# Third head group of a dilated attention kernel: rotated q and k kept in token order, score products read with a step of sixteen words

## The chip, the cores and the metric

The kernel runs on one core of a Trainium2 chip. The metric is the device time of one execution in microseconds (us); the time of a kernel is the median of its runs. A core has TensorE (PE, with its weight loads shown as PEld), VectorE (DVE), ScalarE (ACT), GpSimd (POOL) and SyncE (SP, which here only issues DMAs), and sixteen DMA engines shared by all queues.

## The reference

The reference is one decoder block with two token mixers. Branch A, which the change touches, is causal dilated attention with three head groups of eight heads (head width 64) over 2048 positions. Cut to what matters:

```
DILATION_GROUPS = ((128, 1), (512, 4), (2048, 16))     # (window, dilation)
q = rope(q); k = rope(k)                               # absolute positions 0..2047
for g, (window, dilation) in enumerate(DILATION_GROUPS):
    # positions are regrouped by residue modulo dilation; within a residue
    # the pattern is a band, in blocks of 128 queries
    s = einsum('brnqhd,brnkhd->brnhqk', q_blocks, [previous block, this block] of k) * 64 ** -0.5
    p = exp(s - max(s)); o = p @ v / sum(p)
attn = sum over groups of softmax(log denominators) * o
```

For the third group (dilation 16) a residue has 2048 / 16 = 128 positions, which is one block without a previous one: sixteen blocks per head, each of 128 queries against 128 keys, whose positions lie sixteen apart. All values are float32. Branch B (a gated linear recurrence), the gates, the output projections and the layer norm are as before and after.

## The kernel before, in words

The work has four stages: the input projections (about 0 to 1463 us of the profiled span), the attention (to 1677 us), the projections of both branches, and the output with the layer norm.

**First stage.** The product `x @ W_in` is computed in 72 feature tiles of 128 columns and four token chunks of 512, two feature tiles at a time ("a plan" of pairs, run once for each half of the tokens, by a seven-product scheme on 2x2 blocks). Every float32 operand is split into a high and a low part that TensorE takes at full pace, so each block product is twelve matmuls of 128x512 (L597). `product` and `evacuate` are called once per tick, a tick being one block product. Everything that follows a feature tile (rotation of q and k, gates, recurrence) is a Python generator, a "chain", that gives up control with `yield Ask(...)`. `run_chains` resumes a chain when its lag in ticks is over, when enough of the 32 slots for 128x512 tiles are vacant (`need`), and when the engine budgets of this tick (`DVE=1.2` and the like) are not spent. So numbers in an `Ask` decide in which tick, and therefore in which place of each engine's stream, the work behind it is put. Engines work through their streams in order.

`qk_chain` does the rotation. SP swaps 32-row pieces into `sw`, DVE multiplies by the cosine, POOL by the sine, and a DVE add gives the rotated tile. For the first group the add works in place (`rp = rw`). For groups two and three (`g` is 1 and 2) it writes a new tile `rp`, with the words regrouped by residue: for the third group word `r * 32 + j` of a chunk holds position `16 * j + r`. A rotated k then goes to its scratch array (`k_scr`) as it is. A rotated q is scaled by 0.125 and split into `hi` (ACT) and the remainder (DVE), and both parts go to `qh_scr` and `ql_scr`. For the third group these two DMAs (L331) also gather a residue's words over the four chunks, so that 128 consecutive words of the array are one block; each of their 2048 pieces is 32 words. SP issues them, as it does the loads of the weights (`wA`, `wS`), the stores and loads of the weights' low parts (`wl_scr`, L278 and L283) and the pieces for the rotation (L303).

**Second stage.** There are twelve units, a unit being a pair of heads of one group, in the order group one, group three, group two, four times over. A unit has four iterations `i`, each of four blocks. `unit_parts` loads q's two parts into `A` and k into `B`, and splits k there into its high and low part. An iteration issues on TensorE: 24 score products (L976: four blocks, the three part products high-high, low-high and high-low, two heads on the two halves of the partitions), then the transposes of the previous iteration's probabilities (L1001), then the value products of the iteration before that (L1029). DVE adds the mask and takes the maximum (L983), ACT takes the exponential (L991), and ACT and DVE bring the transposed probabilities from PSUM (L1014, L1016). For the third group the block of q is `A[hs, x, n * P:(n + 1) * P]`, 128 consecutive words, and the block of k is four runs of 32 consecutive words, one of each chunk. These products have 128 moving columns; those of the first group, and most of the second, have 256.

Of the kernel before, what the change touches and what calls it, by code (L numbers as in the profile page):

```python
# [11 lines left out]
ALU = mybir.AluOpType  # L12
# [3 lines left out]
P = 128  # L16
# [4 lines left out]
CH = 512  # L21
# [10 lines left out]
def hybrid_block_kernel(ctx: ExitStack, tc: tile.TileContext, a: dict, out: bass.AP):  # L32
    nc = tc.nc
    sp, act, dve, pool, pe = nc.sync, nc.scalar, nc.vector, nc.gpsimd, nc.tensor

    def flat(t):
        return t.bitcast(F32)
# [14 lines left out]
    qk_scr = {(n, u): dram.tile([P, S], F32, name=f"{n}_scr{u}") for u in range(12) for n in ("qh", "ql", "k")}  # L52
# [77 lines left out]
    def take(name, dt=F32R):  # L130
        if not vacant:
            raise RuntimeError(f"no slot at {now['n']}: {[x[1].name if hasattr(x[1],'name') else x[1] for x in home.values()]} chains {len(chains)}")
        i = vacant.pop(0)
        t = sl_p.tile([P, CH], dt, tag=f"s{i}", name=name)
        home[id(t)] = (i, t)
        return t

    def give(*ts):
        for t in ts:
            vacant.append(home.pop(id(t))[0])  # L140

    def give_sent(*ts):

        for t in ts:
            later(2, lambda t=t: give(t))
# [69 lines left out]
    def tt(eng, out, in0, in1, op):  # L215
        eng.tensor_tensor(out=out, in0=in0, in1=in1, op=op)  # L216
# [71 lines left out]

    CS = {}

    def blocks(t, g):

        return t.rearrange("p (r j) -> p j r", r=4 if g == 1 else 16)

    def qk_chain(rw, f, c):
        isq = f < FT_K
        u = f % 12
        g = u // 4
        nm = f"{f}_{c}"
        yield Ask(need=1)  # L300
        sw = take("sw" + nm)
        for b in range(4):
            sp.dma_start(flat(sw)[32 * b:32 * b + 32], flat(rw)[32 * (b ^ 1):32 * (b ^ 1) + 32])  # L303
        yield Ask(lag=2, DVE=1.2 if c < 2 else 1.0, POOL=1.7)
        cos, sin = CS[c % 2]
        tt(dve, flat(rw), flat(rw), cos, ALU.mult)
        tt(pool, flat(sw), flat(sw), sin, ALU.mult)
        yield Ask(lag=1, need=1 if g else 0, DVE=1.2 if g else 1.0)
        if g == 0:
            rp = rw  # L310
            tt(dve, flat(rp), flat(rw), flat(sw), ALU.add)
            give(sw)
        else:
            rp = take("rp" + nm)
            v, r = "p (j r) -> p j r", 4 if g == 1 else 16
            tt(dve, blocks(flat(rp), g), flat(rw).rearrange(v, r=r), flat(sw).rearrange(v, r=r), ALU.add)
            give(rw, sw)
        if not isq:
            yield Ask()
            sp.dma_start(qk_scr["k", u][:, c * CH:(c + 1) * CH], flat(rp))  # L320
            give_sent(rp)
            return
        yield Ask(need=1, ACT=.66, DVE=.9)
        hi = take("hi" + nm)
        act.activation(hi, flat(rp), AF.Copy, scale=0.125)  # L325
        dve.scalar_tensor_tensor(out=rp, in0=flat(rp), scalar=0.125, in1=flat(hi), op0=ALU.mult, op1=ALU.subtract)
        yield Ask()
        for t, part in ((hi, "qh"), (rp, "ql")):
            dst = qk_scr[part, u]
            if g == 2:  # L330
                sp.dma_start(dst.rearrange("p (r i) -> p r i", r=16)[:, :, 32 * c:32 * c + 32],  # L331
                             flat(t).rearrange("p (r i) -> p r i", r=16))
            else:
                sp.dma_start(dst[:, c * CH:(c + 1) * CH], flat(t))
        give_sent(hi, rp)


# [209 lines left out]
    def result(s, fi, c, bank, u):  # L547
# [10 lines left out]
        if kind in ("qk", "v"):  # L558
            y = take("y" + nm)
            total(flat(y), bank, u, f, sgn, True)  # L560
            start_chain(qk_chain(y, f, c) if kind == "qk" else v_chain(y, sgn, f, c))
        elif kind == "mg":
            y = take("y" + nm, F32)
            total(y, bank, u, f, sgn, False)
            start_chain(mg_chain(y, sgn, f, c))
        elif kind == "ga" or not fi:
            y = take("y" + nm, F32)
            total(y, bank, u, f, sgn, False)
            start_chain(silu_chain(y, sgn, f, c))
        else:  # L570
            i = f - FT_U
            if c == 1 and i in put_off:
                y = take("y" + nm, F32)
                total(y, bank, u, f, sgn, True)
                act.activation(ubs[:, i, 2, 0:3], y[:, CH - 3:CH], AF.Copy)
                start_chain(store_chain(y, u_scr[i]))
                return
            ub = ub_free.pop(0)
            total(ub[:, 3:3 + CH], bank, u, f, sgn, True)
            start_chain(lru(i, c, ub), 7 if c % 2 else 0)  # L580
# [98 lines left out]
    for s, pl in enumerate(plan):  # L679
        if pl[0] and pl[4] == "ug":  # L680
            i = pl[1][1][0] - FT_U
# [79 lines left out]
    def unit(u):  # L761

        return (0, 2, 1)[u % 3], u // 3
# [152 lines left out]
    n = len(where)  # L916
# [30 lines left out]
    def first(i, j):  # L947
        u, q = divmod(i, 4)
        g, _ = unit(u)
        return 0 if prev(g, 4 * q + j) is not None else P  # L950

    def scores(i):
        u, q = divmod(i, 4)
        g, _ = unit(u)
        A, B = units[u]
        if q == 0:
            sta[u] = p_p.tile([P, 16, 4], F32, tag="sta", name=f"sta{u}", bufs=3)
            ot[u] = at_p.tile([P, S], F32, tag="ot", name=f"ot{u}")
        for w in range(2):
            s = st["s", i, w] = [aps.tile([P, 2, 256], F32, tag="s", name=f"s{i}{w}{h}", bufs=4) for h in range(2)]  # L960
            for j in range(2):
                n = 4 * q + 2 * w + j
                lo = first(i, 2 * w + j)
                for x, y in ((0, 0), (1, 0), (0, 1)):
                    for h, hs in enumerate(HALF):
                        K = B[hs, y]
                        if g == 2:
                            k = K.rearrange("p (c r j) -> p r c j", c=4, r=16)[:, n]
                        elif lo:
                            k = K[:, n * P:(n + 1) * P]  # L970
                        elif g == 0:
                            k = K[:, (n - 1) * P:(n + 1) * P]
                        else:
                            c, r = divmod(n, 4)
                            k = K[:, (c - 1) * CH:(c + 1) * CH].rearrange("p (c r j) -> p r c j", c=2, r=4)[:, r]
                        pe.matmul(s[h][:, j, lo:256], A[hs, x, n * P:(n + 1) * P], k, start=(x + y == 0), stop=(y == 1))  # L976

    def peak(i, j, h):
        u, q = divmod(i, 4)
# [111 lines left out]
    for i in range(NG + 3):  # L1091
        u = i // 4
# [9 lines left out]
        if on:  # L1102
            scores(i)
# [193 lines left out]
    for n in range(32):  # L1297
        c, f = divmod(n, 8)
# [147 lines left out]
    for tt in range(16):  # L1446
        c, b = divmod(tt, 4)
# [71 lines left out]
```

## Time and profile before

| | |
|---|---|
| median of three runs | 2148.55 us (2148.51 to 2153.36) |
| the profiled execution's own time | 2152.92 us |
| its span, first to last instruction | 2151.2 us |
| mean granted TensorE clock | 0.996 |
| PE busy | 2101.0 us (98%) |
| PEld busy | 1747.2 us (81%) |
| DVE busy | 1697.1 us (79%) |
| ACT busy | 1081.1 us (50%) |
| POOL busy | 738.4 us (34%) |
| DMA | 525.74 MB in 348266 packets, 123568 of them under 512 B |
| chain that ended last | PE 61% of the span, ACT 6%, DMA 5%, DVE 4% |

Busy time is the union of an engine's instructions. Matmuls overlap, so a matmul's duration in a row is longer than the time from one to the next. In the groups, a row gives busy time and mean duration of one, then the engine's idle time before them and who ended it; a row of a line or a tile gives the least, the median and the greatest duration.

### The profile page before, as it was taken

The numbers are of one execution on the slowest core, as the hardware profiler recorded it, in microseconds if no ns is written. First come the engines' busy times: TensorE is split into PE (matmuls) and PEld (weight loads), VectorE is DVE, ScalarE is ACT, GpSimd is POOL, SyncE is SP. The second block draws the span as 40 slices with busy tenths as digits, with TensorE's granted clock in tenths as the row PEclk, the third lists the DMA queues.
The fourth block names the chain that finished last, engine by engine and source line by source line (L and its number), as shares of the span: only waits on it lengthen the run. The fifth ranks groups of instructions, "written<-read, shape, count | busy, mean of one in ns | idle before, by whom it ended". The sixth has DMA issues, their size and how long they took to land.

```text
span 2151.2 us, 36029 instructions
## 1 busy us (share of the span) xinstructions
PE 2101.0 (98%) x12016; PEld 1747.2 (81%) x12016; DVE 1697.1 (79%) x3009; ACT 1081.1 (50%) x2284; POOL 738.4 (34%) x581
## 2 busy tenths in 40 slices
PE   8999999999999999999999999999999999979998
PEld 6888877888888888888888888887888888868887
DVE  8788888989989977787787887878999545466667
ACT  6354545456356566546657666658999211211100
POOL 1545454654654202121221231224446244321120
PEclk9999999999999999999999999999999999999999
DMA  8888897997997976677788878779898788954431
GB/s 271 255 263 251 249 262 223 271 275 245 279 288 240 306 225 192 221 233 221 233 258 268 267 243 257 244 243 382 284 312 266 232 265 278 306 186 142 164 108 69
DMA packets 348266, 525.74 MB, mean 244 GB/s; under 512 B 123568, under 2 KB 156336, under 8 KB 344240
## 3 DMA queue, kind: packets, MB, share of 16 engines
q1 hardware_dynamic: 330368, 491.64, 70.8%
q0 software_dynamic: 10080, 18.35, 5.4%
q10 hardware_dynamic: 7632, 13.44, 1.8%
q8 instruction: 96, 1.57, 0.3%
q14 instruction: 90, 0.74, 0.1%
HBM read 318.18 MB, written 190.45 MB: 236 GB/s over the span
## 4 chain that ended last, share of the span: by engine, by line
PE 61%; ACT 6%; DMA 5%; DVE 4%; issue 1%; SPq 1%; POOL 0%; DVEq 0%; ACTq 0%; POOLq 0%
PE q L597 39%; ACT p L991 5%; PE z L1389 3%; PE z L1387 3%; PE z L1388 3%; PE yb L1276 2%; PE yb L1277 2%; PE yb L1278 2%; PE o L1029 1%; ACT ptb L1014 1%; PE ya L1354 1%; PE ya L1355 1%; PE ya L1356 1%; PE s L976 1%; DMA yb_scr<-gB 1%
## 5 line engine op out<-in xcount | busy, mean ns | idle before, releaser
L597 PE MATMUL q<-xT,hS 128*128 128x512 f32 x1680 | 519.0, 390 | 0.0
L597 PE MATMUL q<-xT,l 128*128 128x512 f32 x1120 | 436.0, 389 | 0.0
L597 PE MATMUL q<-xB,hA 128*128 128x512 f32 x1248 | 387.4, 391 | 6.3 <-ACT xB L204 5.6
L597 PEld LDWEIGHTS q<-xT,hS 128*128 128x128 f32 x1680 | 314.1, 188 | 64.7 <-ACT hi L325 0.2
L597 PE MATMUL q<-xB,l 128*128 128x512 f32 x904 | 353.5, 391 | 1.2 <-DMA l<-wl_scr 1.1
L597 PEld LDWEIGHTS q<-xB,hA 128*128 128x128 f32 x1248 | 234.0, 188 | 56.2 <-ACT xB L204 5.6
L597 PEld LDWEIGHTS q<-xT,l 128*128 128x128 f32 x1120 | 210.2, 188 | 43.9
L597 PEld LDWEIGHTS q<-xB,l 128*128 128x128 f32 x904 | 170.3, 188 | 38.0 <-DMA l<-wl_scr 1.5
L216 POOL TENSOR_TENSOR S<-S,wA 128x512 f32<-128x512 f32 x35 | 45.7, 1306 | 414.4 <-DVE S L216 333.7
L216 POOL TENSOR_TENSOR sw<-sw,sin 128x512 f32<-128x512 f32 x96 | 161.4, 1687 | 73.8 <-DMA sw<-y 60.8
L261 ACT ACTIVATE hA<-wA 128x512 fp32r<-128x512 f32 x218 | 135.6, 624 | 90.2 <-DMA wA<-in_w_in_dram 41.1
L597 PE MATMUL q<-xB,hS 128*128 128x512 f32 x560 | 174.8, 393 | 3.0 <-DVE v L216 3.0
L597 PE MATMUL q<-xT,hA 128*128 128x512 f32 x560 | 173.3, 390 | 2.4 <-ACT hi L325 1.0
L991 ACT ACTIVATE p<-p,sta 128x256 f32<-128x256 f32 (+1 forms) x384 | 172.1, 455 | 4.6 <-DVE sta L983 3.9
L261 ACT ACTIVATE hS<-S 128x512 fp32r<-128x512 f32 x175 | 109.1, 624 | 92.7 <-DVE S L216 50.2
L216 POOL TENSOR_TENSOR l<-wA,hA 128x512 fp32r<-128x512 f32 x68 | 106.0, 1558 | 80.2 <-ACT hA L261 65.2
L597 PEld LDWEIGHTS q<-xT,hA 128*128 128x128 f32 x560 | 104.6, 188 | 26.1 <-issue 1.4
L597 PEld LDWEIGHTS q<-xB,hS 128*128 128x128 f32 x560 | 104.5, 189 | 25.1 <-issue 4.1
L983 DVE CUSTOM_DVE_ANT_0 p<-s,mask 128x256 f32<-128x256 f32 (+1 forms) x384 | 118.7, 361 | 4.3 <-PE s L976 3.6
L1360 POOL TENSOR_TENSOR me<-gA,ybr 128x512 f32<-128x512 f32 x32 | 51.2, 1610 | 194.6 <-DVE gA L1359 179.8
L216 DVE TENSOR_TENSOR y<-y,cos 128x512 f32<-128x512 f32 x96 | 103.9, 1088 | 16.3 <-DMA sw<-y 16.1
L1389 PE MATMUL z<-wo,ml 128*128 128x512 f32 (+1 forms) x264 | 102.0, 386 | 4.7 <-DVE ml L1373 4.7
(201 smaller groups left out, 4430.1 us busy)
## 6 DMA issues: line engine op xcount, KB each, us to landing
wA<-in_w_in_dram SPq DMA_DIRECT2D x253, 256.0 KB, 4.9
wl_scr<-l SPq DMA_DIRECT2D x105, 512.0 KB, 4.8
l<-wl_scr SPq DMA_DIRECT2D x105, 512.0 KB, 4.9
sw<-y SPq DMA_DIRECT2D x384, 64.0 KB, 3.1
wS<-in_w_in_dram SPq DMA_DIRECT2D x70, 256.0 KB, 4.6
wS<-in_w_in_dram POOLq DMA_DIRECT2D x70, 256.0 KB, 6.3
qh_scr<-hi SPq DMA_DIRECT2D x48, 256.0 KB, 5.1
v_scr<-vs SPq DMA_DIRECT2D x48, 256.0 KB, 4.5
```

The costliest lines, as they stand in the source:

```text
L216: eng.tensor_tensor(out=out, in0=in0, in1=in1, op=op)
L261: act.activation(h, r, AF.Copy)
L597: pe.matmul(bank, w[:, ks], x[:, kk, xx], start=(first and i == 0), stop=(last and i == 11))
L983: dve.tensor_tensor_reduce(out=st["p", i, j][:, h, lo:256], in0=st["s", i, j // 2][h][:, j % 2, lo:256], in1=mask[:, lo:256], scale=1.0, s ...
L991: act.activation(p, p, AF.Exp, scale=-1.0, bias=s[:, h:h + 1], accum_out=s[:, 2 + h:3 + h])
L1276: pe.matmul(yb, WL[f][:, 0, k], xx[:, 0], start=(k == 0), stop=False)
L1277: pe.matmul(yb, WL[f][:, 0, k], xx[:, 1], start=False, stop=False)
L1278: pe.matmul(yb, WL[f][:, 1, k], xx[:, 0], start=False, stop=(k == 7))
L1360: pool.tensor_tensor(out=ME[c][:, f], in0=ga, in1=yb, op=ALU.add)
L1387: pe.matmul(z, mh[:, k], w[:, 0, hs], start=(k == 0), stop=False)
L1388: pe.matmul(z, mh[:, k], w[:, 1, hs], start=False, stop=False)
L1389: pe.matmul(z, ml[:, k], w[:, 0, hs], start=False, stop=(k == 7))
```

## The change

The change is confined to the third group (`g == 2`).

- `qk_chain`: the rotated q and k are no longer regrouped. The add works in place, as for the first group, so there is no tile `rp`; the resumption before it asks for no vacant slot and a DVE budget of 1.0 instead of 1.2. `blocks` falls away, its case for the second group being written out.
- The DMAs of q's two parts write whole rows of 512 words into the scratch arrays; line L331 is gone. What `k_scr`, `qh_scr` and `ql_scr` hold is now in token order.
- `scores`: both operands of the third group's products are read with a step of sixteen words: 128 words of `A` and 128 words of `B`, each word 64 bytes from the last.

```
-        yield Ask(lag=1, need=1 if g else 0, DVE=1.2 if g else 1.0)
-        if g == 0:
+        yield Ask(lag=1, need=1 if g == 1 else 0, DVE=1.2 if g == 1 else 1.0)
+        if g != 1:
             rp = rw
             tt(dve, flat(rp), flat(rw), flat(sw), ALU.add)
             give(sw)
         else:
             rp = take("rp" + nm)
-            v, r = "p (j r) -> p j r", 4 if g == 1 else 16
-            tt(dve, blocks(flat(rp), g), flat(rw).rearrange(v, r=r), flat(sw).rearrange(v, r=r), ALU.add)
+            tt(dve, flat(rp).rearrange("p (r j) -> p j r", r=4), *(flat(t).rearrange("p (j r) -> p j r", r=4) for t in (rw, sw)),
+               ALU.add)
             give(rw, sw)
...
         for t, part in ((hi, "qh"), (rp, "ql")):
-            dst = qk_scr[part, u]
-            if g == 2:
-                sp.dma_start(dst.rearrange("p (r i) -> p r i", r=16)[:, :, 32 * c:32 * c + 32],
-                             flat(t).rearrange("p (r i) -> p r i", r=16))
-            else:
-                sp.dma_start(dst[:, c * CH:(c + 1) * CH], flat(t))
+            sp.dma_start(qk_scr[part, u][:, c * CH:(c + 1) * CH], flat(t))
...
                         if g == 2:
-                            k = K.rearrange("p (c r j) -> p r c j", c=4, r=16)[:, n]
+                            k = K.rearrange("p (j r) -> p r j", r=16)[:, n]
...
-                        pe.matmul(s[h][:, j, lo:256], A[hs, x, n * P:(n + 1) * P], k, start=(x + y == 0), stop=(y == 1))
+                        qn = A[hs, x].rearrange("p (j r) -> p r j", r=16)[:, n] if g == 2 else A[hs, x, n * P:(n + 1) * P]
+                        pe.matmul(s[h][:, j, lo:256], qn, k, start=(x + y == 0), stop=(y == 1))
```

The instructions are as many as before on every engine. Since the chains' asks differ, some of them move by a tick or a few. Two places are shown.

SP's stream near 1296 us of the profiled span, where the last pair of the third group's feature tiles is written out in the second half of the tokens (names: `qh_scr`, `ql_scr`, `k_scr` the scratch arrays, `l` the weights' low parts that the next products need). Before:

```order
L283 DMA l_63_12730<-wl_scr_144 128x512
L331 DMA qh_scr_114<-hi_3_12708 2048x1x32
L331 DMA ql_scr_115<-rp_3_12678 2048x1x32
L320 DMA k_scr_116<-rp_2_12711 128x512
L283 DMA l_64_12770<-wl_scr_145 128x1024
L283 DMA l_64_12816<-wl_scr_145 128x1024
L283 DMA l_64_12863<-wl_scr_145 128x1024
```

Now:

```order
L283 DMA l_63_12702<-wl_scr_144 128x512
L325 DMA qh_scr_114<-hi_3_12679 128x512
L325 DMA ql_scr_115<-y_3_12540 128x512
L316 DMA k_scr_116<-y_2_12571 128x512
L283 DMA l_64_12741<-wl_scr_145 128x1024
L283 DMA l_64_12778<-wl_scr_145 128x1024
L316 DMA k_scr_116<-y_3_12622 128x512
```

The two writes of q's parts keep their place ahead of the loads of `l`, with rows of 512 words instead of 2048 pieces of 32; the other chunk's k comes up between the loads.

DVE's stream at the same place (`y` is the tile that is rotated, in the feature tiles' chunks 2 and 3; `u`, `v` and `S` belong to the projection's scheme). Before:

```order
L216 TENSOR_TENSOR rp_3_12678<-y_3_12568,sw_3_12594 128x32x16
L216 TENSOR_TENSOR y_2_12599<-y_2_12599,cos_7641 128x512
L326 SCALAR_TENSOR_TENSOR rp_3_12678<-rp_3_12678,hi_3_12708 128x512
L216 TENSOR_TENSOR rp_2_12711<-y_2_12599,sw_2_12618 128x32x16
L216 TENSOR_TENSOR u_12713<-e_12687,q_63_12689 128x512
L216 TENSOR_TENSOR y_2_12623<-y_2_12623,cos_7641 128x512
L216 TENSOR_TENSOR y_3_12650<-y_3_12650,cos_7645 128x512
```

Now:

```order
L216 TENSOR_TENSOR y_3_12540<-y_3_12540,sw_3_12566 128x512
L216 TENSOR_TENSOR y_2_12571<-y_2_12571,cos_7625 128x512
L322 SCALAR_TENSOR_TENSOR y_3_12540<-y_3_12540,hi_3_12679 128x512
L216 TENSOR_TENSOR y_2_12571<-y_2_12571,sw_2_12590 128x512
L216 TENSOR_TENSOR y_2_12595<-y_2_12595,cos_7625 128x512
L216 TENSOR_TENSOR u_12685<-e_12658,q_63_12660 128x512
L216 TENSOR_TENSOR y_2_12595<-y_2_12595,sw_2_12617 128x512
L216 TENSOR_TENSOR y_3_12622<-y_3_12622,cos_7629 128x512
```

The adds of the third group become plain 128x512 adds, and the next chunk's multiplication and add come one or more places earlier.

In the attention stage no instruction moves on any engine; TensorE's score products stand where they stood, and only the addresses of their two operands change. In the first stage a few groups of gate products (six matmuls of 128x512) and of transposes stand one or two block products earlier or later.

More of the change, by code (lines that the diff above doesn't have):

```diff
@@ L289, in hybrid_block_kernel @@
     CS = {}
-    def blocks(t, g):
-        return t.rearrange("p (r j) -> p j r", r=4 if g == 1 else 16)
     def qk_chain(rw, f, c):
```

## The prediction

> **What bounds the kernel now.** I first read the busy time by stage (each row: length, then busy time of PE, PEld, DVE, ACT and POOL, with the clock and the DMA share), and the chain of work that ended last.
>
> ```profile
> core 0: us, PE busy (x) PEld busy (x) DVE busy (x) ACT busy (x) POOL busy (x), PEclk, DMA share, GB/s
> 0.00:1463.40 1463.40, 1450.44 (x6456) 1195.25 (x6457) 1216.06 (x1603) 809.84 (x1331) 507.30 (x380) 1.00 0.83 252
> 1463.40:1677.00 213.60, 196.24 (x3555) 178.05 (x3555) 201.00 (x941) 203.70 (x837) 110.42 (x120) 1.00 0.90 298
> ...
> PE 61%; ACT 6%; DMA 5%; DVE 4%; issue 1%; SPq 1%; POOL 0%; DVEq 0%; ACTq 0%; POOLq 0%
> ```
>
> In the first stage PE is busy 1450 of 1463 us; DVE, DMA and SP can give only what PE still waits for. The waits of PE in that stage say how much that is (total, times, longest):
>
> ```profile
> PE q L597 <- ACT xB L204: 5.6, 1, 5.6
> PE q L597 <- DVE v L216: 3.0, 2, 2.6
> PE q L597 <- DVE u L216: 1.1, 4, 0.4
> PE q L597 <- DMA l<-wl_scr: 1.1, 1, 1.1
> PE q L597 <- ACT hi L325: 1.0, 1, 1.0
> PE q L597 <- DVE xT L205: 0.9, 1, 0.9
> ```
>
> They sum to 12.7 us. The 5.6 us are the start, before any rotation; what is left for this change is 7.1 us at most.
>
> In the attention stage PE, DVE and ACT are all busy over 90%, so I read the third group's iterations one by one. This is PE's timeline of the second of its four units (start, duration of the run of equal instructions, idle time before it):
>
> ```profile
> 1533.87 1.56 PE L976 MATMUL s<-B,A 64*128 64x128 f32 x24
> 1535.27 1.18 PE L1001 MATMUL pt<-ident,p 64*128 64x64 f32 x32
> 1536.63 1.97 PE L1029 MATMUL o<-ptb,V 128*64 128x128 f32 x32 [0.19 <-ACT ptb L1014]
> 1538.53 1.56 PE L976 MATMUL s<-B,A 64*128 64x128 f32 x24
> 1539.92 0.68 PE L1001 MATMUL pt<-ident,p 64*128 64x64 f32 x16
> 1540.82 1.97 PE L1029 MATMUL o<-ptb,V 128*64 128x128 f32 x32 [0.22 <-ACT ptb L1014]
> 1542.72 1.56 PE L976 MATMUL s<-B,A 64*128 64x128 f32 x24
> 1544.11 0.68 PE L1001 MATMUL pt<-ident,p 64*128 64x64 f32 x16
> 1545.01 1.09 PE L1029 MATMUL o<-ptb,V 128*64 128x128 f32 x16 [0.22 <-ACT ptb L1014]
> 1546.04 1.56 PE L976 MATMUL s<-B,A 64*128 64x128 f32 x24
> ```
>
> The iterations take 4.66, 4.19 and 3.32 us (differences of the score rows' starts). PE's only idle time in each is about 0.2 us before the value products, and the chain of waits runs through PE in the first two and through ACT after them:
>
> ```profile
> 1536.63 1.97 PE o L1029 x32
> 1538.60 1.49 PE s L976 x24
> ...
> 1544.96 3.08 ACT p L991 x16
> ```
>
> So there are two bounds, PE and ACT, within 0.2 us of each other: any lengthening of these 24 products by more than that moves the end.
>
> **The change part by part.**
>
> *Score products with strided operands.* Four units of four iterations of 24 products: 384 products, with a strided weight load and a strided moving operand each. No operand of TensorE is read with such a step now, so the cost must be bounded by other rows. What the 24 products cost now: from the start of the scores to that of the transposes 1535.27 - 1533.87 = 1.40 us, 58 ns each. Which side of a product sets this, the load of 128 weights or the 128 moving columns?
>
> ```profile
> 1519.46 1.70 PE L976 MATMUL s<-B,A 64*128 64x256 f32 x24
> L976 PEld LDWEIGHTS s<-B,A 64*128 64x128 f32 x1152 | 72.3, 186 | 11.0 <-issue 7.2 <-DVE sta L983 2.2 <-DVE y L216 0.7
> L1029 PEld LDWEIGHTS o<-ptb,V 128*64 128x64 f32 x1200 | 64.5, 137 | 20.9 <-ACT ptb L1014 20.8
> ```
>
> With 256 moving columns instead of 128 (first row, the first group) 24 products take 1.70 us instead of 1.56. Twice the streaming adds 0.14 us, so in the third group the weight load sets the pace, and a moving operand of twice the time would add about 0.14 us. A load of 128 columns lasts 186 ns and one of 64 columns 137 ns: 49 ns for 64 columns, 0.77 ns a word. The first stage streams 512 columns in 1463.40 us / 6456 = 227 ns, 0.44 ns a word. The 256 columns above take 1.70 us / 24 = 71 ns, 0.28 ns a word, which is only possible if the two heads, on the two halves of the partitions, run side by side. So a pair of products has 2 x 58 = 116 ns in the third group, of which a load needs 128 x 0.77 = 99 ns and a stream 128 x 0.44 = 56 ns.
>
> What does a wide step cost elsewhere? DVE's add of the rotation has such a step today: for groups two and three it writes each word 128 or 512 bytes from the last (`rp`), for group one side by side (`y`). Beside it stand two small operations of 128 words, one reading pairs of words 48 bytes apart (L1182), one reading them packed (L1192):
>
> ```profile
> L216 DVE TENSOR_TENSOR rp<-y,sw x64: 1068/1119/2328, 86.0 to 1433.1; 128x512 f32<-128x512 f32 x64
> L216 DVE TENSOR_TENSOR y<-y,sw x32: 673/684/4376, 130.3 to 1109.7; 128x512 f32<-128x512 f32 x32
> L1182 DVE TENSOR_TENSOR wgt<-wmx,stats x3: 286/286/296, 1696.7 to 1697.1; 128x128 f32<-128x128 f32 x3
> L1192 DVE TENSOR_TENSOR wgt<-wgt,wmx x3: 287/288/294, 1705.0 to 1705.4; 128x128 f32<-128x128 f32 x3
> ```
>
> Single words far apart cost 1068 / 512 = 2.09 ns each against 1.31 ns, fixed time included: 1.6 times as long, and if the fixed part overlaps, twice. Pairs cost nothing. It is a write on another engine, so it bounds the price without giving it. From below: a strided word takes no longer than the 0.77 ns that the weight load spends anyway; then only the moving side slows, +0.14 us an iteration, inside the 0.2 us of idle time. From above: 2.09 ns for each word, first the load, then the stream, 128 x 2.09 = 267 ns each (priced among the rivals). Between them I take twice the time for both operands, since the DVE row is nearest to a factor of two: 24 x 58 ns = +1.40 us an iteration. The idle 0.2 us before the value products goes, because their release (ACT's copy `ptb`) no longer comes last: 1.40 - 0.2 = 1.2 us. That holds for the ACT-bound iterations too, where PE has the same 0.22 us. 16 x 1.2 = **+19 us**. Behind the late products stand, on PE, the transposes and value products, and for them DVE's maxima and ACT's exponentials; they have no other work that could fill in, so I let nothing be given back.
>
> [...]
>
> *q's two writes.* SP's own rows, third group (L331) against the others (L334), and the place where a wait of PE hangs on it:
>
> ```profile
> L331 SPq DMA_DIRECT2D qh_scr<-hi x16: 524/580/862, 90.1 to 1312.3; - x16
> L331 SPq DMA_DIRECT2D ql_scr<-rp x16: 623/2787/7050, 90.8 to 1313.1; - x16
> L334 SPq DMA_DIRECT2D qh_scr<-hi x32: 319/382/827, 147.1 to 1432.2; - x32
> L334 SPq DMA_DIRECT2D ql_scr<-y x16: 319/324/1032, 148.6 to 1114.5; - x16
> ...
> 1296.20 3.07 SPq L331 DMA_DIRECT2D ql_scr<-rp  x1
> 1299.36 1.35 SPq L320 DMA_DIRECT2D k_scr<-rp  x1
> 1300.80 1.68 SPq L283 DMA_DIRECT2D l<-wl_scr  x3
> ...
> 1305.83 0.50 PE L597 MATMUL q<-xB,l 128*128 128x512 f32 x1 [1.07 <-DMA l<-wl_scr]
> ```
>
> By the medians SP is freed 16 x (0.20 + 2.46) = 43 us, nearly all of it while PE works. Visible is one case: the load of `l` at 1300.80 stands behind the 3.07 us of `ql_scr`, and PE waits 1.07 us for it. I count that and about as much again for the same delay elsewhere (DVE's `u` and `v` waits): **-2 us**, bounds 0 and -7.1.
>
> *The add.* 32 adds fall from 1119 to 684 ns: 14 us less of DVE in the first stage, covered by PE's 99%. If a DVE wait of PE hangs on them, it is in the 7.1 us. The dropped tile and vacancy ask let chains run a tick earlier; products that move by a block or two find PE full, at 0, with the same bounds. Loads of `A` and `B` are as large as before: 0.
>
> *Sum.* +19 - 2 = +17 us on the profiled execution's 2152.92 us, 2170. That execution is 4.4 us above the median 2148.55, so I add to the median: 2165.5, rounded to 2165 us.
>
> **The rivals.**
>
> *The weight load hides it (not slower).* If a strided word costs up to 0.77 ns, the load stays at 58 ns and the stream at the 256-column pace: +0.14 us, absorbed. For it: the load is by far the slower side now, per word, so a memory fast enough for it is no surprise. Against: the DVE rows. It decides as long as the step costs the load under about 0.2 us / 24 = 8 ns. Time: 2148.55 - 2 = 2147 us.
>
> *A fixed time a word.* If the memory needs 2.09 ns a word whatever the engine, the load alone takes 267 ns; for twelve pairs 12 x (267 - 116) = +1.8 us an iteration, less 0.2: 16 x 1.6 = +26, less 2: 2172 us. Against it: for words side by side DVE's add needs 1.31 ns and PE's stream 0.44 ns, so the two engines share no pace there.
>
> *Load and stream one after the other.* If, besides, the slow load no longer hides beside the slow stream, a pair takes 2 x 267 = 534 ns: 12 x (534 - 116) = +5.0 us, 16 x 4.8 = +77, less 2: 2224 us. For it nothing in the profile; against it that a load of 128 columns hides almost wholly beside a stream of 256 (1.70 us against 1.56).
>
> *The first stage gains more.* No price for the step, and all 7.1 us of waits go: 2141 us. Against: the waits are of five kinds and few hang on the rotation; a reordered stream can as well make new ones.
>
> **How the numbers follow.** Forecast 0.46, hidden behind the load 0.29, fixed time 0.12, one after the other 0.07, first stage gains 0.06. A measurement of this kernel can tell about 0.3%, 6.4 us, from no change. Faster: the last case, 0.06, for it ends just past that. Same: the second, and the forecast's own lower end, where the factor is below 1.5, 0.29 + 0.03 = 0.32. Slower: the rest, 0.62. The forecast's own range is 2155 to 2171 (from a factor of 1.5, 16 x 0.5 - 2, to the full 16 x 1.4 with no idle time used up and nothing from the writes). The range over the cases is 2144 to 2184: it leaves out the first-stage gain, one after the other and some of the tails.
>
> **What would show it.** In the changed profile, the 24 score products of the third group from start to transposes: 2.8 us if I am right, 1.4 to 1.55 if the load hides the step, above 3.2 for a fixed time. The three iterations of the timeline above, 12.2 us now, become 15.8. The weight load's own row should rise from 186 by some 50 ns or more; if it stays and the matmul's rises, the moving side has the cost. `ql_scr` issues should fall to about 0.35 us and the 1.07 us wait for `l` should be gone. I am wrong if the attention stage keeps its 213.6 us, or if the first stage changes by more than 7 us.

## The result and the profile after

The changed kernel takes 2184.74 us (median of four runs, 2182.94 to 2190.51) against 2149.47 us for the kernel before (four runs): a ratio of 1.0165, interval 1.0142 to 1.0188. It is slower by 35 us. The forecast was 2165 us, in a range of 2144 to 2184: right in sign, about 20 us too low, and the measured time lies just above the range.

The changed kernel's profiled execution took 2185.19 us, with a span of 2183.5 us against 2151.2, so 32.3 us are to be found in the traces. First, both by stage (length, then busy time of PE, PEld, DVE, ACT and POOL with the number of instructions, granted clock of TensorE with 1.00 for full speed, DMA share, GB/s). The attention stage is cut at its last value product in both. This is the changed kernel:

```profile
0.00:1454.70 1454.70, 1446.84 (x6456) 1195.85 (x6456) 1209.12 (x1603) 809.89 (x1331) 506.98 (x381) 1.00 0.81 254
1454.70:1699.00 244.30, 226.15 (x3425) 207.58 (x3424) 198.08 (x926) 201.20 (x821) 105.41 (x115) 0.89 0.76 255
1699.00:2183.50 484.50, 464.21 (x2136) 382.56 (x2136) 286.58 (x481) 72.06 (x133) 124.26 (x87) 0.98 0.60 194
```

And the kernel before, cut at the same places (its first stage ends at 1463.40):

```profile
1463.40:1668.60 205.20, 188.24 (x3425) 170.97 (x3424) 195.24 (x926) 199.28 (x822) 102.40 (x111) 1.00 0.91 304
1668.60:2151.20 482.60, 462.27 (x2136) 381.02 (x2136) 285.80 (x481) 71.96 (x133) 128.68 (x92) 0.98 0.60 195
```

The first stage became 8.7 us shorter (1463.4 to 1454.7), the attention stage 39.1 us longer, the rest 1.9 us longer. In the attention stage PE is busy 38 us more for the same 3425 matmuls, while DVE and ACT are busy 2 to 3 us more. And the granted clock of that stage is 0.89 where it was 1.00.

PE's timeline of the unit that the prediction showed, in the changed kernel (start, duration of the run of equal instructions, idle time before it):

```profile
1536.32 2.85 PE L968 MATMUL s<-B,A 64*128 64x128 f32 x24
1538.99 1.17 PE L993 MATMUL pt<-ident,p 64*128 64x64 f32 x32
1540.35 1.97 PE L1021 MATMUL o<-ptb,V 128*64 128x128 f32 x32 [0.18 <-ACT ptb L1006]
...
1544.92 0.68 PE L993 MATMUL pt<-ident,p 64*128 64x64 f32 x16
1545.81 1.97 PE L1021 MATMUL o<-ptb,V 128*64 128x128 f32 x32 [0.22 <-ACT ptb L1006]
...
1551.27 1.98 PE L1021 MATMUL o<-ptb,V 128*64 128x128 f32 x16
1553.18 2.91 PE L968 MATMUL s<-B,A 64*128 64x128 f32 x24
1555.89 1.06 PE L993 MATMUL pt<-ident,p 64*128 64x64 f32 x16
```

The 24 score products take 1538.99 - 1536.32 = 2.67 us to the transposes, where they took 1.40: 111 ns each instead of 58. That is the step that was forecast. But look at the value products: in the third iteration 16 of them take 1.98 us, as long as 32 take one iteration earlier. Before the change 16 took 1.09 us. Sixteen transposes grow from 0.68 to 1.06 us. Neither kind of product was changed. The same iterations by length, with the clock as the last column but two; the last row is the first iteration of the next unit, which belongs to the second group and whose reads were not changed:

```profile
1536.32:1542.24 5.92, 5.74 (x90) 5.43 (x88) 4.31 (x22) 4.53 (x20) 4.55 (x6) 1.00 0.67 241
1542.24:1547.71 5.47, 5.25 (x75) 4.94 (x73) 3.56 (x20) 4.05 (x21) 2.83 (x3) 1.00 0.76 308
1547.71:1553.18 5.47, 5.33 (x60) 4.81 (x58) 3.56 (x20) 3.58 (x18) 0.00 (x0) 0.78 0.76 233
1553.18:1558.91 5.73, 5.68 (x59) 5.17 (x57) 3.56 (x20) 3.57 (x18) 0.00 (x0) 0.50 0.81 115
1558.91:1564.55 5.64, 5.59 (x59) 5.08 (x57) 3.55 (x20) 3.56 (x18) 1.48 (x2) 0.51 1.03 406
```

and in the kernel before:

```profile
1533.87:1538.53 4.66, 4.47 (x91) 4.17 (x89) 4.22 (x22) 4.53 (x20) 0.00 (x0) 1.00 0.61 107
...
1542.72:1546.04 3.32, 3.10 (x59) 2.79 (x57) 2.98 (x18) 2.70 (x14) 3.16 (x4) 1.00 1.03 429
...
1549.38:1552.73 3.35, 3.09 (x59) 2.78 (x57) 3.35 (x21) 3.35 (x19) 0.00 (x0) 1.00 0.81 157
```

The iterations before took 4.66, 4.19, 3.32, 3.34 and 3.35 us. The first two grow by 1.26 and 1.28 us, about the 1.2 forecast. The third, fourth and the next unit's first grow by 2.15, 2.39 and 2.29 us, and there the granted clock is 0.78, 0.50 and 0.51. Cut into slices of 3.41 us, placed so that the clock stays the same within each, the changed kernel shows where it changes:

```profile
1547.40:1550.81 3.41, 3.41 (x46) 3.24 (x44) 1.63 (x9) 1.54 (x8) 0.00 (x0) 1.00 0.48 118
1550.81:1554.22 3.41, 3.27 (x34) 2.75 (x30) 2.62 (x12) 3.08 (x15) 0.00 (x0) 0.50 1.15 285
...
1561.04:1564.46 3.42, 3.37 (x40) 2.95 (x38) 2.40 (x17) 2.62 (x14) 1.39 (x2) 0.50 1.05 432
1564.46:1567.90 3.44, 3.11 (x58) 2.89 (x56) 2.92 (x13) 2.58 (x13) 3.28 (x5) 1.00 0.95 391
```

Between the first and the last of these rows the clock is at half for four slices, 13.7 us, though PE's row is busy 3.27 us or more of each of them. A row that is 96% busy and yet at half clock is what the experiments had to explain.

By units (four iterations each), the third group's four units take 22.28, 22.59, 22.63 and 22.60 us instead of 15.5 each: +28.0 us. The next unit's first iteration takes 5.65 instead of 3.35 us in three of four places: +6.9. The first unit of the stage, of the first group, takes 22.9 instead of 18.5 us: +4.4, a wait that has another cause (the last experiments). Together +39.3, against 39.1 measured. The clock falls during that wait too, to 0.50 for 6.8 us from 1465.5 on.

### The profile page after: what moved, and what is told of

Its sections match the earlier page's. It is cut to its first block, busy times and chain, and to the rows that moved or that the text cites. A ratio compares the mean times of both kernels' runs of the same rounds, so it can differ in the third digit from the quotient of the medians.

```text
span 2183.5 us, 36045 instructions
## 1 busy us (share of the span) xinstructions
PE 2137.2 (98%) x12016; PEld 1786.0 (82%) x12016; DVE 1693.8 (78%) x3009; ACT 1083.2 (50%) x2284; POOL 736.6 (34%) x581
## 4 chain that ended last, share of the span: by engine, by line
PE 62%; ACT 5%; DMA 3%; DVE 2%; issue 1%; SPq 0%; POOL 0%; DVEq 0%; ACTq 0%
PE q L588 37%; ACT p L983 3%; PE s L968 3%; PE z L1381 3%; PE z L1379 3%; PE z L1380 3%; PE o L1021 2%; PE yb L1268 2%; PE yb L1269 2%; PE yb L1270 2%; ACT ptb L1006 1%; PE ya L1346 1%; PE ya L1347 1%; PE ya L1348 1%; DMA yb_scr<-gB 1%; DMA gA<-mg_scr 1%
## 5 line engine op out<-in xcount | busy, mean ns | idle before, releaser
L968 PE MATMUL s<-B,A 64*128 64x256 f32 (+1 forms) x1152 | 108.2, 337 | 5.4 <-DVE sta L975 4.8
L968 PEld LDWEIGHTS s<-B,A 64*128 64x128 f32 x1152 | 97.1, 237 | 16.9 <-issue 6.8
```

Of the source, the lines that this page charges most:

```text
L968: pe.matmul(s[h][:, j, lo:256], qn, k, start=(x + y == 0), stop=(y == 1))
```

## The experiments

The theory after the result had two parts. **Pace**: the strided operands double the time of the score products, PE becomes the bound, and that alone is worth about 20 us. **Clock**: the rest of the loss is the half clock, which comes with it. The rivals: the loss comes from the rest of the change (the order of the first stage, q's writes); only one operand carries the pace; and the half clock comes from the step itself, or merely from longer iterations. Each run is compared with the kernel before on the same chip.

### The change without the step

The changed kernel, reading contiguous words. As no regrouping is left, the third group's scores are of the wrong positions; the amount of work is that of the changed kernel.

```
-  k = K.rearrange("p (j r) -> p r j", r=16)[:, n]
+  k = K[:, n * P:(n + 1) * P]
-  qn = A[hs, x].rearrange("p (j r) -> p r j", r=16)[:, n] if g == 2 else A[hs, x, n * P:(n + 1) * P]
+  qn = A[hs, x, n * P:(n + 1) * P]
```

> The change with the third group's score products reading 128 consecutive words of q and of k instead of every sixteenth; all else as in the changed kernel. The scores are then those of wrong positions: the grouping by residue is left out. My theory (the step costs the products' pace and, by what PE then leaves idle, its granted clock): the 24 products of an iteration take 1.4 us from their start to the transposes, as before the change, the clock in the third group's iterations is 1.0, the four iterations of a unit take 15.5 us, and the whole is 2143 to 2150 us. Rival (the moved order of the first stage or the writes of q cost a part): the time stays above 2160 us.

Measured: 2148.18 against 2149.84 us, ratio 0.9991 (0.998 to 1.0002). One unit of the third group:

```profile
1528.82:1544.33 15.51, 14.62 (x274) 13.39 (x272) 14.03 (x80) 14.61 (x69) 7.40 (x8) 1.00 0.95 306
```

15.51 us and clock 1.00, as before the change. So the step carries the whole loss, and all the rest of the change (plain adds, whole rows of q, the new order) is worth -1.9 us, between -4.3 and +0.4. The first score starts at 1454.93 here, as early as in the changed kernel and 8.5 us earlier than before; the first unit of the attention stage gives back 3.4 of them. The two profiled executions differ by 7.2 us and the medians by only 1.7, since the profiled execution of the kernel before lies above its median and the one of this run below.

### One operand at a time

q alone in token order, so that only the weight load has the step (k is regrouped as before):

```
-  yield Ask(lag=1, need=1 if g == 1 else 0, DVE=1.2 if g == 1 else 1.0)
+  res = 4 if g == 1 else 16 if g == 2 and not isq else 0
+  yield Ask(lag=1, need=1 if res else 0, DVE=1.2 if res else 1.0)
...
+  k = K.rearrange("p (c r j) -> p r c j", c=4, r=16)[:, n]
```

> q of the third group in token order and read with the step of sixteen (the weight load alone); k regrouped and read in runs of 32 words, as before the change. Theory A (the load sets the pace, as the prediction said): nearly all of the cost is here, 24 products take about 2.7 us, the clock falls to half in the later iterations of a unit, 2178 to 2186 us. Theory B (load and stream follow one another and each doubles): 24 products take about 2.05 us, 2155 to 2165 us.

And k alone in token order, so that only the moving operand has the step (q is regrouped and written in pieces of 32 words, as before):

```
+  res = 4 if g == 1 else 16 if g == 2 and isq else 0
...
+  qn = A[hs, x, n * P:(n + 1) * P]
```

> k of the third group in token order and read with the step of sixteen (the moving operand alone); q regrouped and written in pieces of 32 words, as before the change. Theory A (the slower stream hides beside the load): 24 products take 1.4 to 1.55 us and the time is that of before, 2146 to 2152 us. Theory B (each doubles, one after the other): about 2.05 us, 2155 to 2168 us.

Measured: q alone 2192.64 us, ratio 1.0182 (1.0147 to 1.0218); k alone 2150.03 us, ratio 0.9999 (0.9982 to 1.0015). With q's step alone, PE's timeline:

```profile
1544.47 2.86 PE L969 MATMUL s<-B,A 64*128 64x128 f32 x24
1547.17 1.17 PE L994 MATMUL pt<-ident,p 64*128 64x64 f32 x32
```

and one unit by its stretch:

```profile
1544.47:1567.13 22.66, 21.98 (x275) 20.37 (x273) 14.98 (x82) 15.72 (x73) 7.38 (x8) 0.83 0.77 227
```

With k's step alone, PE's timeline:

```profile
1530.60 1.59 PE L974 MATMUL s<-B,A 64*128 64x128 f32 x24
1532.01 1.17 PE L999 MATMUL pt<-ident,p 64*128 64x64 f32 x32
```

and one unit by its stretch:

```profile
1530.60:1546.14 15.54, 14.68 (x274) 13.45 (x272) 13.98 (x80) 14.56 (x69) 7.39 (x8) 1.00 0.96 323
```

The strided weight load alone brings the whole loss of the unit: 2.70 us for the 24 products, a unit of 22.66 us, the same half clock. The time of q alone lies above the 2178 to 2186 us that were expected, and 8 us above the changed kernel. In its profile the clock is at half in the first iteration behind all four units of the third group, not three, and the first unit of the attention stage takes 26.5 us instead of 22.9, since DVE waits 7.6 us there for writes of the gates (the last experiments). The strided moving operand costs nothing here: 1.41 us, a unit of 15.54. The weight load's own row in this timeline's unit tells it as well. First of the kernel before, then of the changed one (min/median/max in ns of the 24 loads):

```profile
L976 PEld LDWEIGHTS s<-B,A x24: 183/188/188, 1533.9 to 1535.1; 64*128 64x128 f32 x24
```

```profile
L968 PEld LDWEIGHTS s<-B,A x24: 291/307/307, 1536.3 to 1538.7; 64*128 64x128 f32 x24
```

### The pace without a step

The kernel before with each of the third group's score products issued twice, with the regrouped operands of before. The second pass starts the sum anew, so the output stays what it was.

```
-  for x, y in ((0, 0), (1, 0), (0, 1)):
+  for x, y in ((0, 0), (1, 0), (0, 1)) * (2 if g == 2 else 1):
```

> The kernel before, with every score product of the third group issued twice from consecutive words (48 instead of 24 an iteration, the second set overwriting the first). PE then needs about as long for them as with the step, 2.7 us an iteration, but works on every word at full pace. Theory (the granted clock falls because the strided products leave PE little active): the clock stays 1.0 through the third group and the time is 2149 + 16 x (1.3 - 0.2) = 2166 us, 2162 to 2171 us. Rival (the clock falls with the longer iterations themselves, or the cost has nothing to do with the clock): the clock falls here too and the time is 2178 us or more.

Measured: 2172.41 us, ratio 1.0098 (1.0076 to 1.012), so +21 us. PE's timeline:

```profile
1540.47 2.90 PE L976 MATMUL s<-B,A 64*128 64x128 f32 x48
1543.20 1.18 PE L1001 MATMUL pt<-ident,p 64*128 64x64 f32 x32
```

and one unit by its stretch:

```profile
1540.47:1561.32 20.85, 20.00 (x372) 18.76 (x370) 14.38 (x80) 14.85 (x69) 7.38 (x8) 1.00 0.71 229
```

48 products without the step take 2.73 us, a little more than the 24 strided ones (2.67 us). The unit takes 20.85 us, as do the third group's other three, and the clock stays at 1.00 in all of them. So score products twice as long are worth 5.3 us a unit, 21 us in all, and the changed kernel's units of 22.6 us hold 1.8 us more than that. But here the array also streams twice the words in that time, so this run does not yet say whether the step itself or the few words streamed bring the clock down.

### The same load with a wider stream

q's step alone, as above, and every product of the third group streams 256 contiguous words of k instead of 128, into the half of the score tile that the third group leaves unused. The scores are of the wrong positions.

```
-  k = K.rearrange("p (c r j) -> p r c j", c=4, r=16)[:, n]
+  k = K[:, 256 * (n // 2):256 * (n // 2) + 256]
-  pe.matmul(s[h][:, j, lo:256], qn, k, start=(x + y == 0), stop=(y == 1))
+  pe.matmul(s[h][:, j, 0 if g == 2 else lo:256], qn, k, start=(x + y == 0), stop=(y == 1))
```

> As q_step (weight load with the step of sixteen), but each product streams 256 consecutive words of k instead of 128, into the half of the scores' tile that the third group leaves unused; k's words are those of wrong positions. The load's cost stays, but TensorE streams twice as much in the same time. Theory (the granted clock falls because the array stands nearly idle beside the slow loads): 24 products still take 2.7 to 2.9 us, the clock stays 1.0 through the third group, and the time is 2164 to 2174 us. Rival (the clock falls with strided loads as such, or with the longer iterations): the clock is 0.5 in each unit's later iterations as in q_step, 2180 to 2195 us.

Measured: 2173.38 us, ratio 1.0105 (1.0086 to 1.0123): more words through PE, and by the ratios about 17 us less than q's step alone. PE's timeline:

```profile
1538.57 2.93 PE L969 MATMUL s<-B,A 64*128 64x256 f32 x24
1541.34 1.15 PE L994 MATMUL pt<-ident,p 64*128 64x64 f32 x32
```

and the unit, with the next unit's first iteration below it, by stretches:

```profile
1538.57:1559.48 20.91, 20.06 (x276) 18.83 (x274) 14.39 (x80) 14.86 (x69) 7.41 (x8) 1.00 0.76 228
1559.48:1562.82 3.34, 3.09 (x59) 2.78 (x58) 3.34 (x21) 3.34 (x19) 0.00 (x0) 1.00 0.91 211
```

The loads are as slow as with 128 words (24 products in 2.77 us), the unit as long as by pace alone (20.85 us above), and the clock stays at 1.00. So it does in the other three units, of 20.90 or 20.91 us, and in every run of this kernel the mean granted clock is 0.993 or 0.994, against 0.979 to 0.989 with q's step alone. So neither the slow load nor the length of the iterations is enough to bring the clock down. What is left, as I read these runs, is how little the array streams while it waits for its weights: behind a load of this pace the clock fell with 128 words (0.83 over the unit with q's step alone) and was kept with 256 (1.00). Two things limit this reading. The 256 words are also contiguous, where q's step alone had four runs of 32; the run with every product issued twice kept the clock with such runs, but 128 contiguous words behind a strided load were not run. And 128 words do not always lose the clock: in the run with a step of eight words below, whose products are slower still, one of the four units keeps it:

```profile
1603.86:1625.60 21.74, 20.90 (x275) 19.67 (x273) 14.38 (x80) 14.85 (x69) 7.37 (x8) 1.00 0.78 250
```

What decides it from unit to unit is not shown.

The difference to the changed kernel's units, 22.28 + 22.59 + 22.63 + 22.60 - 4 x 20.91 = 6.5 us, and the 6.9 us of the units that follow, are the price of the clock: 13.4 us. It is rather too low, by up to 16 x 0.1 = 1.6 us, since the 24 products with 256 words take 0.1 us longer than the changed kernel's.

### From which step on

The changed kernel with both operands read at a step of 2, 4 and 8 words instead of 16 (scores of the wrong positions), one run each:

```
+  k = K.rearrange("p (b j r) -> p b r j", j=P, r=S)[:, n // S, n % S]
+  qn = A[hs, x].rearrange("p (b j r) -> p b r j", j=P, r=S)[:, n // S, n % S] if g == 2 else ...
```

> The changed kernel with both operands of the third group's products read with a step of 2 words instead of 16 (words of wrong positions). [...] If any step costs: 2.7 us, about 2185 us.

> The same with a step of 4 words, so one word of each 16 bytes. [...] If the limit is at a wider step (32 or 64 bytes): 1.4 us, about 2150 us.

> The same with a step of 8 words. [...] If the cost grows with the step, between those of steps 4 and 16.

Measured: 2150.43, 2183.97 and 2184.71 us. PE's timeline with a step of two words:

```profile
1538.33 1.67 PE L968 MATMUL s<-B,A 64*128 64x128 f32 x24
1539.82 0.68 PE L993 MATMUL pt<-ident,p 64*128 64x64 f32 x16
```

and of four:

```profile
1538.31 3.06 PE L968 MATMUL s<-B,A 64*128 64x128 f32 x24
1541.18 1.92 PE L993 MATMUL pt<-ident,p 64*128 64x64 f32 x32
```

The 24 products take 1.49 us at a step of two words (8 bytes), 2.87 at four, 2.97 at eight (1540.45 to 1543.42) and 2.67 at sixteen. Nearly nothing, and then all of it at once: the cost does not grow with the step. For the weight load it begins between a step of two words (1.49 us) and one of four (2.87); the moving operand, behind a load that sets the pace, shows no cost even at sixteen (1.41 us with k's step alone). Why it begins there no run shows.

### Pairs of words, and the wait at the stage's start

The step-of-two result asks for a version: k in token order (its step of 16 is free), and q regrouped by pairs of residues, so that the rotation writes two words side by side, the writes go out in pieces of 64 words, and the weight load reads with a step of two.

```
+  tt(dve, flat(rp).rearrange("p (m j e) -> p j m e", m=8, e=2),
+     *(flat(t).rearrange("p (j m e) -> p j m e", m=8, e=2) for t in (rw, sw)), ALU.add)
...
+  qn = A[hs, x].rearrange("p (m j e) -> p m e j", m=8, e=2)[:, n // 2, n % 2] if g == 2 else ...
```

> q of the third group regrouped by pairs of residues: two words side by side, read by the weight load with a step of two words; its writes are in pieces of 64 words instead of 32; k in token order and read as the moving operand with the step of sixteen. By step2 and k_step both reads are nearly free; by the two-word rows DVE's adds fall to about 0.7 us. Theory (the first stage is bound by PE): as before the change or a little faster, 2144 to 2151 us, 24 products take 1.45 to 1.55 us. Rival (the pieces of the writes and DVE's relief count): below 2143 us.

Measured: 2145.21 us (twelve runs), ratio 0.9979 (0.9968 to 0.9989): it is faster than the kernel before by some 4.5 us. Its 24 products take 1.49 us (1528.54 to 1530.03). One unit:

```profile
1528.54:1544.41 15.87, 15.01 (x275) 13.77 (x274) 14.15 (x80) 14.70 (x69) 7.41 (x8) 1.00 0.93 308
```

The step of two costs 0.36 us a unit, 1.4 us in all. The first score starts at 1457.56, 5.8 us earlier than before, and here nothing is given back at the start of the attention stage.

In the changed kernel something is. PE's timeline there, in the first unit of the attention stage:

```profile
1466.46 1.99 PE L968 MATMUL s<-B,A 64*128 64x256 f32 x12 [4.59 <-DVE sta L975]
```

and the wait of DVE that stands behind it (total, times, longest; ACT's copies wait 3.6 us for the same):

```profile
DVE ptb L1008 <- DMA mg_scr<-y: 4.4, 1, 4.4
```

`ptb`, the copies of the transposed probabilities, waits for the last writes of the gates (`mg_scr`) out of tiles `y`. The attention stage's tiles take the places in SBUF that those tiles leave, and they are still being written out when the first stage ends 8.7 us earlier. I tried to mend that in the changed kernel, and in the version with pairs, by giving the tiles of the first stage's last steps the free place of the highest number instead of the one that has been free longest:

```
-  i = vacant.pop(0)
+  i = vacant.pop(vacant.index(max(vacant)) if now["n"] >= base[NQ - 1] else 0)
```

> The changed kernel, whose tiles of the last tick group take the slots with the highest numbers instead of those longest vacant. In the changed kernel the attention's first copies (ptb) wait 4.4 us for the last stores of gate tiles (mg_scr). Theory (those stores still read slots on which the attention stage puts its first tiles): the wait is gone or moves, the first unit's four iterations take 18.5 us instead of 22.9, and the whole is 2176 to 2183 us. Rival (the stores themselves are late, wherever the tiles lie): the wait stays and the time too, 2183 to 2187 us.

> The same as pairs with the last tiles in the highest slots, as in after_hi. If the first stage's gain is given back at the attention's start by waits for stores, this one keeps it: 2142 to 2147 us, two to five less than pairs. If pairs has no such wait, the two are equal.

Measured: 2193.2 us, ratio 1.0195 (1.0171 to 1.0218), and 2158.45 us, ratio 1.0042 (1.0027 to 1.0056). Both are slower than the versions they should mend, and outside what was expected of them. The waits near the end of the first stage, in the changed kernel with the highest places:

```profile
DVE u L216 <- DMA mg_scr<-y: 9.6, 1, 9.6
PE s L968 <- issue: 8.4, 1, 8.4
```

The wait on `mg_scr` goes where the places go, to DVE's `u` in the projection's scheme, and becomes longer. The first unit of the attention stage, freed of it, takes 19.2 us instead of 22.9, but starts 12.5 us later. So the wait comes with the reuse of places; other places than these would have to be taken, and none better was found.

## Why the prediction was wrong

**What bounds the kernel.** Right. PE and ACT were within 0.2 us of each other in the third group's iterations, and with the products longer PE is the bound alone. The chain of waits in the changed kernel now runs through PE's runs of products one after the other (start, duration):

```profile
1601.66 1.97 PE o L1021 x32
1603.63 2.78 PE s L968 x24
```

**The price of the step: +19 us.** Right in size, and right that the load sets the pace: the 24 products take 2.67 us, forecast as 2.8, and by unstrided products of about that length it is +21 us. The factor of two itself was luck: it was chosen between wide bounds from a write on DVE, and nothing on PE spoke for it (the load's own row grew by a factor of 1.6, from 188 to 307 ns). The two small rows beside it do not show that pairs of words cost nothing, as was read: both write pairs 24 bytes apart, and L1192 reads such pairs too, so pairs stand against pairs. The version with pairs shows it, where the adds into `rp`, which now hold the third group's q in pairs beside the second group's single words, take 676 ns at least, against 1068 at least before, when all wrote single words. Two details of the price were not right either. The step was priced for both operands, but the load has all of it. And the 0.2 us of idle time before the value products were counted as used up; in the first two iterations of the timeline they stand there as before (0.18 and 0.22), since ACT's copy begins later too. That is why the iterations grow by nearer to 1.3 us than to 1.2.

**Nothing behind the late products.** This is the step that failed: "they have no other work that could fill in, so I let nothing be given back" took it that the transposes and value products start later and run as long as before. They run longer. From the third iteration on the granted clock falls to half, 16 value products take 1.98 instead of 1.09 us, and the fall outlasts the unit. That is worth 13.4 us, and it is no term of the sum and no rival. The column of the granted clock was read as 1.00 by stage, and what holds it there was not asked. It is the clock that takes the time past the range's upper end; the run with the pace alone, at 2172 us, lies inside. Of the rest of the miss, about 2 us are the pace (21.5 by the units instead of 19), and about 3 us lie between the difference of the two profiled executions (32.3) and that of the medians (35.3).

**q's writes and the first stage: -2 us.** By net effect right (-1.9 us without the step, -4.3 to +0.4), by place not, so the agreement is luck. The forecast capped the gain at 7.1 us of waits; the first stage gained 8.7. PE's waits there in the changed kernel (total, times, longest):

```profile
PE q L588 <- ACT xB L204: 5.6, 1, 5.6
PE q L588 <- DVE u L216: 1.0, 1, 1.0
PE q L588 <- DVE xT L205: 0.9, 1, 0.9
PE q L588 <- DVE v L216: 0.3, 1, 0.3
```

The wait of 1.1 us for `l` is gone, as said, and that for `v` falls from 3.0 to 0.3. The waits fall by 4.9 us, inside the cap. But PE is also busy 3.6 us less for the same 6456 matmuls, and that the cap left out: a wait of PE here cost more than its length. The 2.6 us for `v` in the kernel before stand here, in PE's timeline,

```profile
332.49 0.70 PE L597 MATMUL q<-xB,hS 128*128 128x512 f32 x2 [2.62 <-DVE v L216]
```

and behind them the clock was at half (0.50) for 3.4 us, from 333.3 on, which by my estimate is worth about half of that, 1.7 us; the changed kernel has no such stretch in its first stage. The other 1.9 us of busy time I have not traced. Then 4.4 us were given back at the stage's boundary, a place that the prediction didn't look at. `ql_scr` issues fell to a median of 383 ns (0.35 us forecast).

**The rivals.** "The weight load hides it" is wrong for the load and right for the other half of its argument: the moving side is hidden (0.9999 with k's step alone). "A fixed time a word" asked for more than 3.2 us for the 24 products, and "one after the other" for 6.4; both fall with 2.67. "The first stage gains more" happened, with 8.7 us, but the next stage gave 4.4 of them back.

Of the signs named, the products' time, the load's row (188 to 307 ns) and `ql_scr` came as said. The three iterations came to 16.9 us instead of 15.8, the clock's part. The first stage moved by more than the 7 us that were named as a failure.

## What to carry to other kernels

Read a weight load's fp32 words with a step of one or two (24 products in 1.40 and 1.49 us here); steps of four, eight and sixteen paid the full price (2.87, 2.97 and 2.67 us), and three was not tried. The moving operand's step of sixteen words cost nothing behind the load that sets the pace (1.41 us, ratio 0.9999). Before making TensorE's products longer without giving them more to stream, ask whether the granted clock will hold (it fell to 0.50 here with 128 words, and stayed at 1.00 with 256), and price the products that stand behind them at half clock too (1.98 instead of 1.09 us for 16 value products). And a stage that ends earlier gains only what the next stage's tiles, taken from the same places, allow: in the changed kernel 4.4 of 8.7 us were given back.

## What the runs showed that was not expected

PE's row was 96% busy (3.27 of 3.41 us) while its clock was at half: in the changed kernel 24 products an iteration that wait for strided loads and stream 128 words each bring it to 0.50 some 15 us after the first of them (1536.3 to 1550.8 in the unit shown), the same loads with 256 words keep it at 1.00. At a step of eight words one unit of four kept it with 128 words as well. The stretches at half clock measured above, 6.8 and 13.7 us in the changed kernel, are two and four times the 3.4 us of the one in the kernel before. What sets their length no run shows; a busy row in the profile did not keep the clock up.

The pace of the strided load does not follow the granted clock. At half clock the 24 strided products take the same 2.7 us (1553.18 to 1555.89) as at full clock (2.67), while value products behind them take 1.98 instead of 1.09 us. So the load's time did not lengthen with the half clock; what it waits for no run shows.
